# Two-layer diffusion trunk: softmax weights transposed in row halves, another spread of the convolution's taps, and later sums of a norm

## The chip, the cores and the metric

The kernel runs on one core of a Trainium2 chip. The metric is the time of one execution on the device in microseconds (us), the median of several runs. The engines are PE (TensorE: matmuls, with PEld for its weight loads), DVE (VectorE), ACT (ScalarE), POOL (GpSimd) and SP (SyncE, which issues the transfers here). Each runs its own list of instructions in order and waits for others by semaphores. Results of PE go to PSUM, eight banks of 128 partitions x 2 KB; everything else stands in SBUF.

## The reference

A trunk of two layers over 256 latent tokens and 256 context tokens, width 1024. Each layer mixes tokens by a convolution branch and an attention branch with gates, and then has a gated MLP. Cut to what matters:

```python
for l in range(DEPTH):                       # DEPTH = 2; the last layer: latent tokens alone
    h = modulate(rmsnorm(x, norm1_g[l]), sh1, sc1)
    p = h @ w_in[l]                          # columns: GLU, q, k, v, gates
    u = a * sigmoid(g)                       # a, g: halves of the GLU columns (512 each)
    u = dwconv1d(u, dw, dw_b)                # 31 taps per channel, along the tokens
    y_conv = silu(layernorm(u, ln_g, ln_b)) @ w_conv_out[l]
    s = concatenate([q @ k_window + bias, q @ k_ctx])     # 8 heads of 64
    y_attn = softmax(s) @ concatenate([v_window, v_ctx]) @ w_na_out[l]
    g_conv, g_attn = split(sigmoid(p_gate))
    x = x + g1 * ((g_conv * y_conv + g_attn * y_attn) @ w_out[l])
    h2 = modulate(rmsnorm(x, norm2_g[l]), sh2, sc2)
    x = x + g2 * conv_ffn(h2, w_up, dw3, dw3_b, w_down)
    # the same for the context tokens in layer one, with attention among themselves
return rmsnorm(x, final_norm_g)
```

## The kernel before, in words

Activations stand transposed, channels on the 128 partitions and tokens along the row: 256 latent tokens (`LAT`), then 256 context tokens (`CTX`). Layer one (index 0 in the code) has both, rows of T = 512; layer two (index 1, `last`) has T = 256. `S` is 256, `P` 128, `KD` 8, `KC` 4.

**Weights.** They come in units of 128 x 1024 from memory by SP (`wunit`, L155: tile `raw`, four buffers) and are split into a high part (ACT, L158, `whi`) and a low part (DVE, L159, `wlo`) in a rounded fp32 format, as is every activation. A product is three matmuls (`mm3`, L177 to L179: high x high, high x low, low x high). So ACT and DVE work for each unit that PE is to use, and a `raw` buffer is free when DVE has read it. SP's list also holds the units of the modulation's weights (`raw_unit`, L145) and two rows of the condition (`across`, tile `sb`, L243), which ACT puts through Silu (L245).

**Work between groups.** The main program on PE is a row of groups (8 k-steps of `mm3`). After halves or wholes of groups it calls `slot()`, which moves each generator in a list (`side`) one step on: the attention, the convolution's taps, its norm, the dots of the modulation on DVE (`ada_dots`, L261, custom instructions of 128 x 1024). The tile framework then decides each engine's order and its waits from the order in which the instructions were written, with `tc.issue_after` as extra constraints.

**Convolution.** `glu(j, ..)` writes tile `u` for channels j (four of them) and puts its 31 taps into the list `taps`. `conv_tap` is one DVE instruction (L576: `cb = u * w + cb`, 128 x 512 in layer one, 128 x 256 in layer two), 124 in each layer with the four first ones. `conv_run` gives `rate[0]` taps per slot. In layer one there were two `u` tiles, `us[j % 2]`, so `glu` first ran the taps that still read the tile it is to write. When the attention is over, `layer_norm` (L815) takes the rest in portions, then forms the mean (sum on POOL and DVE, a matmul with ones on PE, L832), subtracts it (L835), forms squares on ACT and their sums on DVE (L308, L312), lets PE sum over the channels (`rstd`, L326), DVE scale (`root`, L334), POOL take the power -0.5 (L336), PE spread it over the partitions (L341), and DVE and ACT normalise (L843 to L847). It yields between the steps, so its place on PE follows from the slots.

**Attention.** A step of `Attention.step` takes, in this order: the turn of the step before (L476), the values of the turn before that (L494), and the score products of the next pair of heads (L430), which use 64 rows of the array for each head, the two heads in the two row halves and in two banks. ACT and DVE then do the softmax (L448 to L454) into tiles `pp`, queries on partitions, keys along the row. The values need keys on partitions, so a *turn* transposes four `pp` tiles of 128 x 512: 16 transposes of 128 x 128 on PE (L484 for latent queries, L489 for context queries), into the banks `sc`, `sc`, `pt`, `main`, one for each `pp`, and four copies of 128 x 512 on ACT into `pT` (L485, L490). Then `values` (L502) multiplies by `V` into `po`, with 64 columns of the array for each head. Layer one has six turns (four latent, two context), layer two four: 160 transposes.

**The second norm of layer two.** After the residual (L883) the first four groups of the MLP run on `h2` without the factor of the norm (`plain`, L893 and L894), interleaved over k with its sums: at k = 2 `next(sums)` issues L326 and L334, at k = 4 `whole(sums)` the spread L341. The modulation of `h2` follows on DVE and ACT (L355 to L357), the first groups are scaled afterwards (L1000), and the next two groups read the modulated tiles. PE's work after L341 in these loops is what the modulation has for cover.

## Time and profile before

| what | value |
|---|---|
| median of three runs | 1130.06 us (1129.4 to 1134.78) |
| span of the profiled execution, from the first to the last instruction | 1127.4 us |
| granted TensorE clock, mean | 0.998 |
| layer one's attention, about | 80 to 203 us |
| layer two's turns | 813 to 861 us |
| layer two's second norm | 933 to 945 us |

The profile is of one execution. Its page gives busy times of the engines (PE's ends are modelled), the chain of work that ended last, followed back from the last instruction, and groups of instructions, each named by line, engine, operation and tile, with the count, busy time and mean in ns of one. `out<-in` are the program's tile names. In a timeline a row has start, length and name, and in brackets how long its engine stood idle before it and what released it. Two of the chain's kinds, `PEld` and `PE`, overlap: a weight load runs under the matmul before it. The execution's time outside the span isn't in the profile; 1130.06 and 1127.4 stand 2.7 us apart.

### The profile page before, as it was taken

The page shows a single profiled execution, that of the slowest core. Times are in us where ns is not written, and L with a number is a line of the kernel's source. Part 1 is how long each engine was busy: PE and PEld are TensorE (multiplying, and loading weights), DVE is VectorE, ACT ScalarE, POOL GpSimd, SP SyncE. Part 2 cuts the span into 40 slices and gives each one's busy share as a digit, 9 for nine tenths or more (in the row PEclk, how much of TensorE's full clock was granted, in tenths as well). Part 3 has the DMA queues.
Part 4 walks back from the last instruction along what each step waited for, and adds up shares of the span by engine and source line. Part 5 has one row for each costly group of instructions (what it writes and reads, how often), then busy time and mean ns, then how long its engine had stood idle before and what let it go on. Part 6 is the DMA issues. An engine that isn't in the chain of part 4 may idle for free.

```text
span 1127.4 us, 17780 instructions
## 1 busy us (share of the span) xinstructions
PE 1115.5 (99%) x6854; PEld 965.1 (86%) x6854; DVE 906.5 (80%) x1625; ACT 565.7 (50%) x937; POOL 17.2 (2%) x24
## 2 busy tenths in 40 slices
PE   9999999999999999999999999999999999999997
PEld 7678777787789988888888888989898999999997
DVE  4689999786778788888898555789996898988773
ACT  4347657542334543444334223544677667766642
POOL 0000000000000000000000000010000000000000
PEclk9999999999999999999999999999999999999999
DMA  8832231635734354545556656555533575665781
GB/s 325 310 100 89 92 117 38 200 99 198 248 120 145 110 170 133 184 152 155 165 181 205 214 188 197 176 194 174 154 109 120 180 247 175 187 193 182 213 274 57
DMA packets 53941, 190.83 MB, mean 169 GB/s; under 512 B 6240, under 2 KB 6496, under 8 KB 53856
## 3 DMA queue, kind: packets, MB, share of 16 engines
q1 hardware_dynamic: 53568, 189.65, 52.6%
q8 instruction: 54, 0.88, 0.3%
q14 instruction: 31, 0.25, 0.1%
q10 hardware_dynamic: 288, 0.04, 0.0%
HBM read 188.62 MB, written 1.05 MB: 168 GB/s over the span
## 4 chain that ended last, share of the span: by engine, by line
PE 85%; DVE 10%; DMA 2%; ACT 2%; issue 1%; POOL 0%; SPq 0%; DVEq 0%; ACTq 0%; POOLq 0%
PE main L177 25%; PE main L179 24%; PE main L178 24%; DVE cb L576 4%; PE main L629 4%; DVE wlo L159 2%; DMA raw<-in_wall 1%; PE sc L127 1%; PE sc L177 1%; PE sc L179 1%; PE sc L178 1%; PE po L200 1%; PE po L502 1%; DMA sb<-in_crow 1%; PE sc L430 0%
## 5 line engine op out<-in xcount | busy, mean ns | idle before, releaser
L177 PE MATMUL main<-h,whi 128*128 128x256 f32 (+1 forms) x1328 | 446.8, 337 | 0.0
L179 PE MATMUL main<-h,wlo 128*128 128x256 f32 (+1 forms) x1328 | 443.4, 335 | 0.5 <-DVE wlo L159 0.5
L178 PE MATMUL main<-h,whi 128*128 128x256 f32 (+1 forms) x1328 | 442.4, 333 | 0.0
L158 ACT CAST whi<-raw 128x1024 fp32r<-128x1024 f32 (+1 forms) x244 | 252.5, 1039 | 284.7 <-PE main L178 128.6
L159 DVE TENSOR_TENSOR wlo<-raw,whi 128x1024 fp32r<-128x1024 f32 (+1 forms) x244 | 293.7, 1209 | 113.3 <-ACT whi L158 108.6
L177 PEld LDWEIGHTS main<-h,whi 128*128 128x128 f32 x1328 | 249.5, 188 | 32.0 <-issue 3.9
L179 PEld LDWEIGHTS main<-h,wlo 128*128 128x128 f32 x1328 | 249.5, 188 | 28.9 <-DVE wlo L159 0.7
L178 PEld LDWEIGHTS main<-h,whi 128*128 128x128 f32 x1328 | 249.9, 188 | 28.1 <-issue 0.2
L576 DVE SCALAR_TENSOR_TENSOR cb<-u,par,cb 128x512 f32<-128x512 f32 (+1 forms) x240 | 140.6, 620 | 1.2
L261 DVE CUSTOM_DVE_ANT_0 t<-raw,sb,par 128x1024 bf16<-128x1024 f32 x100 | 126.9, 1280 | 1.4 <-ACT sb L245 1.2
L177 PE MATMUL main<-fh,whi 128*128 128x256 f32 (+1 forms) x386 | 123.0, 319 | 0.0
L178 PE MATMUL main<-fl,whi 128*128 128x256 f32 (+1 forms) x386 | 122.9, 319 | 0.0
L179 PE MATMUL main<-fh,wlo 128*128 128x256 f32 (+1 forms) x386 | 122.9, 318 | 0.0
L178 PEld LDWEIGHTS main<-fl,whi 128*128 128x128 f32 x386 | 72.7, 188 | 5.6
L177 PEld LDWEIGHTS main<-fh,whi 128*128 128x128 f32 x386 | 72.7, 188 | 5.6
L179 PEld LDWEIGHTS main<-fh,wlo 128*128 128x128 f32 x386 | 72.7, 188 | 5.5
L948 ACT ACTIVATE t<-main,par 128x512 f32<-128x512 f32 (+1 forms) x82 | 50.7, 669 | 35.3 <-PE main L179 35.3
L949 DVE SCALAR_TENSOR_TENSOR t<-main,par,t 128x510 f32<-128x510 f32 (+1 forms) x82 | 47.6, 616 | 8.2 <-ACT t L948 7.6
L952 DVE SCALAR_TENSOR_TENSOR t<-main,par,t 128x510 f32<-128x510 f32 (+1 forms) x82 | 46.6, 611 | 0.0
L356 ACT ACTIVATE h<-t,mod 128x256 fp32r<-128x256 f32 x56 | 25.2, 502 | 37.5 <-DVE t L355 37.4
L883 DVE SCALAR_TENSOR_TENSOR x<-main,mod,x 128x256 f32<-128x256 f32 x48 | 22.1, 480 | 23.6 <-PE main L179 23.4
L629 PE MATMUL main<-whi,h 128*128 128x512 f32 x128 | 40.6, 402 | 0.0
(217 smaller groups left out, 1198.0 us busy)
## 6 DMA issues: line engine op xcount, KB each, us to landing
raw<-in_wall SPq DMA_DIRECT2D x239, 512.0 KB, 4.2
raw<-in_wada SPq DMA_DIRECT2D x88, 512.0 KB, 4.4
bias<-in_bias_t SPq DMA_DIRECT2D x8, 640.0 KB, 4.4
row<-in_wada SPq DMA_DIRECT2D x8, 512.0 KB, 4.8
sb<-in_crow SPq DMA_DIRECT2D x5, 512.0 KB, 6.1
x<-in_xt SPq DMA_DIRECT2D x8, 256.0 KB, 4.6
raw<-in_wall SPq DMA_DIRECT2D x8, 256.0 KB, 6.8
out<-t SPq DMA_DIRECT2D x3, 256.0 KB, 2.1
```

The costliest lines, as they stand in the source:

```text
L158: act.copy(hi[:, c], r[:, c])
L159: dve.tensor_tensor(lo[:, c], r[:, c], hi[:, c].bitcast(F32), ALU.subtract)
L177: pe.matmul(ps, w[0], xh, start=start, stop=False)
L178: pe.matmul(ps, w[0], xl, start=False, stop=False)
L179: pe.matmul(ps, w[1], xh, start=False, stop=stop)
L261: dve.tensor_tensor_reduce(tmp().bitcast(BF16), r, v, 1.0, pr(l, BADA + n, 1), ALU.mult, ALU.add, mods[l][:, n, s : s + 1])
L356: high = act.activation(hi[:, c], y[:, c], AF.Identity, bias=b)
L576: dve.scalar_tensor_tensor(cb[j], src, w, cb[j], ALU.mult, ALU.add)
L629: pe.matmul(pv[t], h1[n == 1][k][:, c], w[n == 2][:, b], start=k + n == 0, stop=k == KD - 1 and n == 2)
L948: act.activation(c, pv_, AF.Identity, bias=pr(l, FDB + t, 1), scale=w[1])
L949: dve.scalar_tensor_tensor(c[:, :, 1:], pv_[:, :, : S - 1], w[0], c[:, :, 1:], ALU.mult, ALU.add)
L952: dve.scalar_tensor_tensor(c[:, :, : S - 1], pv_[:, :, 1:], w[2], c[:, :, : S - 1], ALU.mult, ALU.add)
```

## The change

1. **Turns.** Each 128 x 128 transpose becomes two of 64 x 128: the weights are rows 0 to 63 or 64 to 127 of `pp` and the moving operand is the 64 x 64 block of the identity on the same rows, so that 64 queries come out as 64 columns. The two halves of a block go to two banks, written in turn: a bank now holds one half of the queries for both heads of the pair (before: all 128 queries of one head). Both banks of a pair of heads get full together, after 16 halves, and then come their two copies. The copies are still four per turn with 512 columns, in stretches of 64. `pT` is one tile for both heads, two buffers, in place of two tiles with four.
2. **Taps.** Layer one has four `u` tiles (`NU_ = KC`), so `glu` forces no taps. `conv_run` counts with a fraction, 1.75 taps per slot in layer one in place of 2, and the norm takes 3 of the rest per slot in place of 5. Layer two keeps 3 and 6.
3. **Second norm.** In layer two `next(sums)` stands at k = 4 in place of 2, `whole(sums)` at k = 6 in place of 4.
4. **Scratch.** The program is built with `dynamic_dma_scratch_size=1024`, which leaves more of SBUF to the tiles.

In the compiled order layer one's mean L832 moves from place 1094 to 1334 on PE; 96 of these places are the added halves. Behind it come 27 matmuls up to L326 as before, and then 6 up to L341 (21 before).

```diff
-            pts = [self.eb.tile([P, 4, S], F32, tag="pT", bufs=4, name=nm("pT")) for _ in range(2)]
+            pT = self.eb.tile([P, 2, 4, S], F32, tag="pT", bufs=2, name=nm("pT"))
             for n, tags in enumerate((("sc", "sc"), ("pt", "main"))):
+                outs = [psum(t).rearrange("p (i s q) -> p i s q", i=2, s=4) for t in tags]
                 for i, pp in enumerate(pps[n]):
-                    pt = psum(tags[i])
+                    for s in range(4):
+                        src = s if what == LAT else s % 2 * 2 + s // 2
+                        for pt, r in zip(outs, HALF):
+                            pe.transpose(pt[:, i, s], sl(pp, src)[r], ident[r, r])
+                for pt, r in zip(outs, HALF):
                     if what == LAT:
-                        for kt in range(4):
-                            pe.transpose(sl(pt, kt), sl(pp, kt), ident)
-                        act.copy(pts[i][:, :, n * P : (n + 1) * P], pt.rearrange("p (k q) -> p k q", k=4))
+                        act.copy(pT[:, :, :, n * P + r.start : n * P + r.stop], pt)
                     else:
...
-                            pts[i][:, 2 * n + kt - kts[0], :], start=kt == kts[0], stop=kt == kts[-1],
+                            pT[:, i, 2 * n + kt - kts[0]], start=kt == kts[0], stop=kt == kts[-1],
...
-            NU_ = KC if last else 2
+            NU_ = KC
...
-            rate = [0]
+            rate = [0.0]
             def conv_run():
+                due = 0.0
                 while True:
-                    for _ in range(rate[0]):
+                    due += rate[0]
+                    while due >= 1:
+                        due -= 1
                         if taps:
                             conv_tap(*taps.pop(0))
                     yield
...
-                rate[0] = 3 if last else 2
+                rate[0] = 3 if last else 1.75
...
-                        for _ in range(6 if last else 5):
+                        for _ in range(6 if last else 3):
...
-                    if k == 2:
+                    if k == 4:
                         next(sums)
-                    if k == 4:
+                    if k == 6:
                         pb = whole(sums)
...
-    nc = bacc.Bacc("TRN2", target_bir_lowering=False, num_devices=1)
+    nc = bacc.Bacc("TRN2", target_bir_lowering=False, num_devices=1, dynamic_dma_scratch_size=1024)
```

More of the change, by code (lines that the diff above doesn't have):

```diff
@@ L476, in turn, with values @@
         def turn(self, what, its, pps):
-            pts = [self.eb.tile([P, 4, S], F32, tag="pT", bufs=4, name=nm("pT")) for _ in range(2)]
+            pT = self.eb.tile([P, 2, 4, S], F32, tag="pT", bufs=2, name=nm("pT"))
             for n, tags in enumerate((("sc", "sc"), ("pt", "main"))):
+                outs = [psum(t).rearrange("p (i s q) -> p i s q", i=2, s=4) for t in tags]
                 for i, pp in enumerate(pps[n]):
-                    pt = psum(tags[i])
+                    for s in range(4):
[3 more added lines that the diff above has]
+                for pt, r in zip(outs, HALF):
                     if what == LAT:
-                        for kt in range(4):
-                            pe.transpose(sl(pt, kt), sl(pp, kt), ident)
-                        act.copy(pts[i][:, :, n * P : (n + 1) * P], pt.rearrange("p (k q) -> p k q", k=4))
-                    else:
-                        for t in range(2):
-                            for kt in range(2):
-                                pe.transpose(pt[:, kt * S + t * P : kt * S + (t + 1) * P], sl(pp, 2 * t + kt), ident)
-                        act.copy(pts[i][:, 2 * n : 2 * n + 2, :], pt.rearrange("p (k q) -> p k q", k=2))
+                        act.copy(pT[:, :, :, n * P + r.start : n * P + r.stop], pt)
+                    else:
+                        to = pT[:, :, 2 * n : 2 * n + 2].rearrange("p i k (t q) -> p i (k t) q", t=2)
+                        act.copy(to[:, :, :, r], pt)
             js = [its[0][0]] if what == LAT else [it[0] for it in its]
-            self.pv.append((what, js, pts))
-        def values(self, what, js, pts, bank):
+            self.pv.append((what, js, pT))
+        def values(self, what, js, pT, bank):
             po = psum(bank)
```

## The prediction

> **What bounds the kernel now.** Views in this order: the page's head and chain, the windows of the stages that hold the ten turns, then the chain of waits in layer one.

> ```profile
> span 1127.4 us, 17780 instructions
> PE 1115.5 (99%) x6854; PEld 965.1 (86%) x6854; DVE 906.5 (80%) x1625; ACT 565.7 (50%) x937; POOL 17.2 (2%) x24
> PE 85%; DVE 10%; DMA 2%; ACT 2%; issue 1%; POOL 0%; SPq 0%; DVEq 0%; ACTq 0%; POOLq 0%
> ```

> TensorE is busy for 99% of the span, so time taken off PE counts in full wherever nothing else holds the stage. DVE's 10% of the chain says that somewhere it does (columns: PE, PEld, DVE, ACT, POOL, clock, DMA share, GB/s):

> ```profile
> core 0: us, PE busy (x) PEld busy (x) DVE busy (x) ACT busy (x) POOL busy (x), PEclk, DMA share, GB/s
> 84.00:112.00 28.00, 28.00 (x139) 22.18 (x137) 27.63 (x65) 20.06 (x39) 0.00 (x0) 1.00 0.27 89
> 112.00:140.00 28.00, 28.00 (x174) 22.05 (x173) 27.93 (x53) 20.20 (x45) 0.00 (x0) 1.00 0.32 99
> 140.00:170.00 30.00, 30.00 (x151) 23.71 (x151) 30.00 (x62) 17.79 (x31) 1.69 (x1) 1.00 0.37 110
> 170.00:200.00 30.00, 30.00 (x183) 23.46 (x183) 29.53 (x54) 24.05 (x57) 1.30 (x1) 1.00 0.12 36
> ...
> 872.00:900.00 28.00, 28.00 (x236) 27.95 (x236) 22.38 (x49) 16.92 (x36) 0.71 (x1) 1.00 0.58 188
> ```

> Between 84 and 200 us, layer one's attention, DVE idles 0.37 + 0.07 + 0.00 + 0.47 = 0.9 us in 116. Behind layer two's turns it has 28.00 − 22.38 = 5.6 us to spare. The chain of waits, and a line of PE's timeline, show where layer one's DVE work reaches PE:

> ```profile
> 198.98 0.75 DVE cb L576
> ...
> 200.73 1.15 DVE wlo L159
> ...
> 202.27 6.08 DMA sb<-in_crow
> ...
> 212.03 0.44 PE pt L224 x2
> ```

> ```profile
> 212.03 0.44 PE L224 MATMUL pt<-ident,t 128*128 128x128 f32 x2 [1.13 <-ACT t L217]
> ```

> A row of taps (L576), then the low part of a weight unit (L159), whose buffer SP's queue waits for; behind that the load of the context row, its two Silu on ACT, the copy L217 queued behind them, and PE's transpose L224, which stands 1.13 us. This is PE's longest stall. PE has only 1.13 us to give there before every microsecond gained earlier becomes waiting.

> **Edit 1, the turns.** It takes out 16 transposes in each of 10 turns and puts in 32 halves. Per turn before, from the chain of the first one: 0.87 / 8 = 109 ns each, 16 × 109 = 1.74 us.

> ```profile
> 102.85 0.87 PE sc L484 x8
> ```

> No row shows a half transpose. The nearest are the score products, which also run on row halves, into two banks (PE's, then the weight loads' timeline):

> ```profile
> 849.32 0.39 PE L430 MATMUL main<-qk,qk 64*128 64x512 f32 x1
> 849.55 0.39 PE L430 MATMUL pt<-qk,qk 64*128 64x512 f32 x1
> 849.55 0.39 PE L430 MATMUL main<-qk,qk 64*128 64x512 f32 x1
> 849.87 0.39 PE L177 MATMUL main<-h,whi 128*128 128x256 f32 x1
> ```

> ```profile
> 849.09 0.18 PEld L430 LDWEIGHTS pt<-qk,qk 64*128 64x128 f32 x1
> 849.09 0.18 PEld L430 LDWEIGHTS main<-qk,qk 64*128 64x128 f32 x1
> ```

> ```profile
> L326 PEld LDWEIGHTS pt<-one,ss 128*128 128x128 f32 x32 | 4.2, 190 | 1.5 <-DVE ss L312 1.0 <-PE sc L178 0.4
> L484 PEld LDWEIGHTS sc<-ident,pp 128*128 128x128 f32 x64 | 7.4, 141 | 0.8
> ```

> Both matmuls of a pair start together, both loads start together, and the pair steps by 849.55 − 849.32 = 0.23 us. So halves on different rows run side by side. A pair of half transposes moves 64 columns instead of 128: bound to the good side 109 / 2 + 3 ns = 57 ns, if it is the moving columns that set the 109. They seem to: the sums L326 move one column per load and take 0.79 / 8 = 99 ns each (row below), and a transposed load is 190 − 141 = 49 ns shorter than theirs, so about 50 ns. Middle bound: the pair costs what one transpose costs, 109 ns, if two loads of 50 ns don't overlap. Bad bound: the halves run one after the other at full price, 218 ns. I take 57, by the score rows, which show both kinds of overlap; the four instructions would then issue every 14 ns, which no row shows.

> [...]

> A turn then costs 16 × 57 = 0.91 us, 0.83 less. Against it: the values that follow 8 of the 10 turns (L502) run in 128 rows, so PE changes mode once more. Such a change shows above as 849.87 − 849.55 = 0.32 against 0.23, so 0.09 us. Where score products follow at once (the first turn of each layer) there is no extra change, but they wait for the copy of their bank, which now starts only when both banks of a pair are full:

> ```profile
> L485 ACT COPY pT<-sc 128x512 f32<-128x512 f32 x16 | 8.5, 587 | 0.0
> ```

> Two copies of 0.59 us stand between the turn and its banks, so I count these two turns at a gain of 0.2 at best and a loss of 0.4 (one rope copy comes between in layer two). Eight turns gain 0.74 each: five in layer one, three in layer two.

> *Layer one:* 5 × 0.74 = 3.7 us, and it doesn't pass. DVE's order in the changed program has the same L159 ahead of the context row, with one tap more before it (118 against 117), 0.75 us by the row above. DVE was full, so L224 comes 0.7 us later (bounds 0 and 1.0), and PE's stall there grows by about 4.4. Layer one: **+0.7**.

> *Layer two:* 3 × 0.74 = 2.2, less 0.2 for its first turn and 0.5 for weights that DVE splits just in time: **−1.5** (bounds −2.4 and 0).

> **Edit 2, tiles and taps.** Two more memsets on POOL, busy 2%, before any u is written, and no transfer: nothing. The tap count is the same 120; only their places change (counted above). But three leftover taps per slot instead of five, and no forced taps, put the convolution's norm later: its mean (L832) moves some 144 matmuls back on PE, into the groups of the next branch, where slots come twice as often. Before:

> ```profile
> 229.19 0.86 PE po L832 x2
> ...
> 236.32 0.79 PE pt L326 x8
> ...
> 242.09 0.44 PE po L341 x4
> ```

> ```profile
> 235.09 0.69 DVE L312 TENSOR_TENSOR ss<-ss,t 128x512 f32<-128x512 f32 x1
> 235.69 1.28 DVE L261 CUSTOM_DVE_ANT_0 t<-raw,sb,par 128x1024 bf16<-128x1024 f32 x1
> ```

> ```profile
> 237.39 1.99 POOL L336 TENSOR_TENSOR rs<-red,mhalf 128x4 f32<-128x4 f32 x1 [48.62 <-DVE red L334]
> ```

> Before, the squares end at 235.09 + 0.69 = 235.8, 6.6 us behind L832's start, and PE comes 7.1 behind it. After, one dot L261 more stands between the squares: 6.6 + 1.3 = 7.9 against about 7.1 to 7.2 of PE work, a stall of 0.7. Then from L326 to L341 PE had 21 products (4.9 us) over the power on POOL; after only 6, 6 × 0.23 = 1.4. The reduction L334 stands behind another L261 (0.5 us beyond the 0.79 of L326), then takes 0.2, and POOL 1.5 to 2.0: 2.2 to 2.7 against 1.4, a stall of 0.8 to 1.3. Together **+1.8** (bounds 0, if the products queued later have shrunk some other wait, and +4, if the dots find their weights late and L312 waits for two of them). What reads the normed tiles stands about 16 us of PE work behind, so nothing more is late. Where DVE has no dots the cover would be enough and the cost nothing.

> **Edit 3, the second norm's sums** go two steps of k back. PE's stall (first row) is covered: the sums come 24 products of 0.12 us later.

> ```profile
> 933.87 0.61 PE L326 MATMUL pt<-one,ss 128*128 128x1 f32 x4 [0.50 <-DVE ss L312]
> ```

> ```profile
> 937.48 0.22 PE po L341 x2
> ```

> ```profile
> 943.74 0.89 DVE L357 SCALAR_TENSOR_TENSOR h<-t,mod,h 128x256 fp32r<-128x256 f32 x2 [0.19 <-ACT h L356]
> ```

> But the modulation behind L341 also starts about 2.1 us later, and its last L357 ends near 944.6 + 2.1 = 946.7, while the groups that read it start three steps of k, 36 products of 0.12 us, behind L341 (937.7 + 4.3 = 942.0). In the changed order two groups take turns over k, so the last k is first read near 947. I take **−0.3** (bounds −0.5, all of the stall, and +2.2, if the last tile is waited for).

> **Edit 4, the smaller scratch for transfers.** Every load here is issued from SP; I cost it at nothing, and no cover hides it.

> **Sum:** 0.7 − 1.5 + 1.8 − 0.3 = +0.7 on a span of 1127.4, so 1128.1. The median of the runs, 1130.06, stands 2.7 above the span: **1130.8 us**. A change under 0.5% (5.7 us) can't be told from none here.

> **The rivals.**

> *The whole gain passes* (30%). If L224 isn't held by DVE in the changed program, because the context row is loaded earlier or fewer taps per slot bring L159 forward, layer one keeps 3.7 us and may lose up to the 1.13 of stall too. −3.7 − 1.1 − 2.2 − 0.3 and, with the norm's waits covered, 0 for edit 2: −7.3, **1122.8**. For it: POOL and ACT have room, and 1.75 taps leave a quarter of one per slot to other DVE work. Against it: DVE's 0.9 us of idle time, and the same work in front of L159.

> *The halves run one after the other* (12%): slower. Place: the 16 pairs of each turn; price 218 − 109 = 109 ns a pair, 1.74 us a turn. Layer one's 10.5 us less 1.1 of the stall is 9.4, layer two's 7.0, with 0.8 of mode changes, 1.8 and −0.3: +18.7, **1149**. It decides from a pair of about 145 ns on, where the sum passes +5.7. For it: both halves write the same 64-column stretch of two banks, and none of the shown pairs is a transpose. Against it: the score pairs.

> *The pair costs what the whole cost* (10%): no gain, 0.7 + 0.7 of mode changes + 1.8 − 0.3 = +2.9, **1133**. [...]

> *The norm of layer one costs more* (6%): the dots, loaded in turn with the weights, hold L312 and L334, and sh and sl come late for the products that read them; +4 there and 16 us of cover used up by about 3 more: 0.7 − 1.5 + 7 − 0.3 = +5.9, **1136**. It decides once DVE in that stretch is over 90% busy.

> **How the numbers follow.** The forecast has 42%, about 1126 to 1134 by its own bounds. Faster by over 0.5%: the whole gain passing, 30%. Slower: serial halves 12%, the larger norm 6%, a little of the forecast's upper bound 3%: 21%. Within 0.5%: 49%. The range of 8 in 10 reaches down to 1121 and up to 1141, leaving out the serial halves and what is below the full gain.

> **What would show it.** Half transposes 57 ns a pair, a turn near 0.9 us (edit 1's price); L224's stall at 4 to 6 us, with DVE still full before 200 us (swallowed); stalls of about 1 us each at L326 and L341 of the convolution's norm; no stall before the sums near 936. I am wrong if L224 comes earlier than 212, or a turn takes over 1.7 us.

## The result, and the profile after

The changed kernel takes 1143.64 us (median of 5 runs, 1142.8 to 1149.65), the kernel before 1131.22 in the same comparison: a ratio of 1.012, interval 1.0094 to 1.0146. It is slower by some 12 us; forecast were 1130.8, and the range ended at 1141.

The page of the profiled execution, head and chain:

```profile
span 1147.9 us, 18102 instructions
PE 1124.2 (98%) x7014; PEld 965.9 (84%) x7014; DVE 908.4 (79%) x1625; ACT 564.9 (49%) x937; POOL 18.2 (2%) x26
PE 79%; DVE 14%; ACT 4%; DMA 2%; issue 2%; SPq 0%; POOL 0%; DVEq 0%; ACTq 0%; POOLq 0%
```

The chain's share of PE has fallen by 6 points, those of DVE and ACT have risen by 4 and 2: PE waits for both. This execution lost some 3 us at the start, so the readings below are from a second profile of the same kernel (run e4_again: 1143.87 us, span 1142.1). Lines of kernel.py stand 1 to 4 lower there: L485 is the half transpose (L484 and L489 before), L488 its copy, L836 the mean (L832), L839 the centring (L835).

The starts of the same instructions of PE in both profiles say where the time went (the difference is the second profile's start less the one before):

| instruction on PE | before, us | changed, us | difference |
|---|---|---|---|
| L127, end of the start-up | 17.71 | 18.19 | +0.5 |
| L502, values in layer one | 180.53 | 179.72 | -0.8 |
| L502, values after the last context turn | 194.34 | 196.85 | +2.5 |
| L224 | 212.03 | 214.92 | +2.9 |
| L200, products of the modulation behind the norm | 298.04 | 309.30 | +11.3 |
| L326, first norm of layer two | 737.19 | 749.96 | +12.8 |
| L502, last values of layer two | 868.07 | 881.45 | +13.4 |
| L179, behind layer two's second norm | 973.49 | 988.12 | +14.6 |

These are differences of two single executions and add up to 14.6 us, where the medians stand 12.4 apart. The largest part, 8.4 us, lies between 215 and 309 us; in between PE has the same products in both kernels. Windows of the kernel before and then of the changed one (columns as in the prediction):

```profile
230.00:260.00 30.00, 30.00 (x137) 24.44 (x136) 27.93 (x44) 13.98 (x21) 1.99 (x1) 1.00 0.39 120
260.00:300.00 40.00, 40.00 (x221) 30.01 (x220) 22.66 (x39) 9.30 (x13) 0.00 (x0) 1.00 0.63 212
```

```profile
170.00:200.00 30.00, 27.57 (x195) 20.34 (x193) 29.69 (x54) 22.73 (x53) 1.65 (x1) 0.94 0.14 42
200.00:230.00 30.00, 29.73 (x148) 22.50 (x147) 24.31 (x37) 16.59 (x24) 0.00 (x0) 1.00 0.60 211
230.00:260.00 30.00, 30.00 (x130) 24.22 (x130) 9.67 (x13) 7.42 (x11) 0.00 (x0) 1.00 0.40 123
260.00:300.00 40.00, 34.40 (x173) 24.82 (x173) 31.68 (x57) 12.40 (x19) 2.00 (x1) 0.96 0.47 155
```

From 230 to 260 us DVE does 9.7 us of work where it did 27.9, while PE is full and seems fine. The bill comes in the next window: PE idles 5.6 us of 40, and its clock falls to 0.96; with the 1.7 us that this costs (below) that is most of the 8.4. DVE's timeline of the changed kernel, then SP's:

```profile
252.50 1.23 DVE L159 TENSOR_TENSOR wlo<-raw,whi 128x1024 fp32r<-128x1024 f32 x1 [4.36 <-ACT whi L158]
266.45 2.48 DVE L839 SCALAR_TENSOR_TENSOR cb<-po,cb 128x512 f32<-128x512 f32 x4 [12.72 <-PE po L836]
```

```profile
253.75 17.79 SPq L145 DMA_DIRECT2D raw<-in_wada  x2
271.65 0.37 SPq L155 DMA_DIRECT2D raw<-in_wall  x1
```

DVE has reached the centring of the convolution's norm and stands 12.7 us, because PE comes to the mean that late. Everything behind the centring in DVE's list stands with it. By then SP had run ahead and filled the four `raw` buffers: two with dots (loads at 237.6 and 253.8) that DVE reads behind the centring, from 269.4 on, and two with units of the modulation's products L200 (242.6 and 248.2) that PE reads at 270.5. So no buffer came free, and SP stood from 254 to 271 us (the first row of SP's list holds two loads, issued at 253.75 and 271.22, with the wait between them):

```profile
SPq L145 <- PE sc L200: 18.4, 3, 17.1
```

It is the L200 on PE that ends the wait; in the kernel before, the same pair was loaded at 256.4 and 257.5, and while PE had yet to read it, a split on DVE freed another buffer, so that the next pair came ahead: its first unit was loaded at 265.9, its second at 269.7, as soon as PE had read the first of the old pair. Here the next pair is loaded at 276.1 and 280.8, and PE gets to it too early. What PE waited for between 100 and 310 us, in the changed kernel (total, times, longest):

```profile
PE sc L200 <- DMA raw<-in_wada: 4.4, 2, 3.8
PE pt L485 <- ACT pp L472: 2.2, 1, 2.2
PE sc L430 <- ACT pT L488: 1.1, 2, 0.9
PE po L341 <- POOL rs L336: 0.8, 1, 0.8
PE main L177 <- DVE g L874: 0.3, 1, 0.3
PE pt L224 <- ACT t L217: 0.3, 1, 0.3
```

The first row is that pair. L341 is the stall that was forecast at 0.8 to 1.3. The forecast stall at L224 is nearly gone: PE had lost the time before, at L485 and L430.

After two of these stalls the clock is granted at half. Windows of the changed kernel around the stall of L485 and the one of L200:

```profile
192.00:196.00 4.00, 1.63 (x28) 1.04 (x26) 3.96 (x7) 3.50 (x13) 1.65 (x1) 1.00 0.00 0
196.00:200.00 4.00, 3.97 (x25) 2.17 (x25) 3.81 (x6) 3.97 (x7) 0.00 (x0) 0.57 0.00 0
```

```profile
280.00:284.00 4.00, 0.64 (x8) 0.16 (x8) 4.00 (x8) 1.34 (x2) 0.00 (x0) 1.00 0.54 153
284.00:288.00 4.00, 3.46 (x14) 2.25 (x15) 4.00 (x6) 2.27 (x4) 0.00 (x0) 0.59 0.80 246
```

4 us at 0.57 and 4 us at 0.59 each lose 4 x 0.42 = 1.7 us of PE work beyond the stall itself; PE is shown busy all the while.

Last, the turn. PE's timeline has pairs of halves:

```profile
179.20 0.22 PE L485 MATMUL main<-ident,pp 64*128 64x64 f32 x1
179.26 0.22 PE L485 MATMUL pt<-ident,pp 64*128 64x64 f32 x1
179.26 0.22 PE L485 MATMUL main<-ident,pp 64*128 64x64 f32 x1
```

The two halves of a pair start together and the next pair 0.06 us later; the whole turn has its first half at 178.59 and its last pair at 179.57, 0.98 / 15 = 65 ns a pair. The halves are nearly as fast as forecast: the second turn of layer one takes 1.14 us up to the values (112.46 to 113.60) where it took 1.84 (112.00 to 113.84). What became of the 0.70 us, on ACT in the kernel before and in the changed one:

```profile
111.97 1.05 ACT L158 CAST whi<-raw 128x1024 fp32r<-128x1024 f32 x1
113.03 1.28 ACT L591 ACT_TABLE_LOAD   x1
114.33 0.60 ACT L591 ACTIVATE t<-main 128x512 f32<-128x512 f32 x1
114.82 1.07 ACT L485 COPY pT<-sc 128x512 f32<-128x512 f32 x2
```

```profile
112.94 1.04 ACT L158 CAST whi<-raw 128x1024 fp32r<-128x1024 f32 x1
114.00 1.28 ACT L595 ACT_TABLE_LOAD   x1
115.29 0.60 ACT L595 ACTIVATE t<-main 128x512 f32<-128x512 f32 x1
115.79 1.07 ACT L488 COPY pT<-sc 128x512 f32<-128x512 f32 x2
```

```profile
116.42 1.46 PE L430 MATMUL sc<-qk,qk 64*128 64x256 f32 x12 [0.87 <-ACT pT L488]
```

ACT does the same list in the same time, one split, a table load and a sigmoid ahead of the copies; before, PE's score products began at 115.72, as the copies of their banks came to an end. The 0.70 us become a wait (0.87 us by the profile; ACT's list also starts 1.0 us later here, 0.5 of it by the later start of PE). At this turn the copies weren't late because two banks fill together; they were never waiting for PE.

### The profile page after: what moved, and what is told of

Read it like the earlier page. It is cut to its first block, busy times and chain, and to the rows that moved or that the text cites. A ratio compares the mean times of both kernels' runs of the same rounds, so it can differ in the third digit from the quotient of the medians.

```text
span 1147.9 us, 18102 instructions
## 1 busy us (share of the span) xinstructions
PE 1124.2 (98%) x7014; PEld 965.9 (84%) x7014; DVE 908.4 (79%) x1625; ACT 564.9 (49%) x937; POOL 18.2 (2%) x26
## 4 chain that ended last, share of the span: by engine, by line
PE 79%; DVE 14%; ACT 4%; DMA 2%; issue 2%; SPq 0%; POOL 0%; DVEq 0%; ACTq 0%; POOLq 0%
PE main L177 23%; PE main L179 23%; PE main L178 22%; DVE cb L577 6%; PE main L633 4%; DVE wlo L159 3%; PE sc L127 1%; PE sc L177 1%; PE sc L179 1%; PE sc L178 1%; ACT whi L158 1%; PE po L200 1%; DMA raw<-in_wada 1%; DMA sb<-in_crow 1%; DVE sc L448 1%
## 5 line engine op out<-in xcount | busy, mean ns | idle before, releaser
L177 PE MATMUL main<-h,whi 128*128 128x256 f32 (+1 forms) x1328 | 446.5, 337 | 0.0
L179 PE MATMUL main<-h,wlo 128*128 128x256 f32 (+1 forms) x1328 | 442.8, 335 | 1.1 <-DVE wlo L159 1.1
L178 PE MATMUL main<-h,whi 128*128 128x256 f32 (+1 forms) x1328 | 442.3, 334 | 0.1
L159 DVE TENSOR_TENSOR wlo<-raw,whi 128x1024 fp32r<-128x1024 f32 (+1 forms) x244 | 293.3, 1208 | 111.4 <-ACT whi L158 106.6
L177 PEld LDWEIGHTS main<-h,whi 128*128 128x128 f32 x1328 | 249.4, 188 | 32.2 <-issue 4.4
L179 PEld LDWEIGHTS main<-h,wlo 128*128 128x128 f32 x1328 | 249.3, 188 | 29.7 <-DVE wlo L159 1.5
L178 PEld LDWEIGHTS main<-h,whi 128*128 128x128 f32 x1328 | 249.8, 188 | 28.6 <-DVE h L357 0.5
L261 DVE CUSTOM_DVE_ANT_0 t<-raw,sb,par 128x1024 bf16<-128x1024 f32 x100 | 127.0, 1279 | 8.4 <-DMA raw<-in_wada 6.9
L177 PE MATMUL main<-fh,whi 128*128 128x256 f32 (+1 forms) x386 | 123.0, 319 | 0.0
L178 PE MATMUL main<-fl,whi 128*128 128x256 f32 (+1 forms) x386 | 122.9, 319 | 0.0
L179 PE MATMUL main<-fh,wlo 128*128 128x256 f32 (+1 forms) x386 | 122.9, 318 | 0.0
L178 PEld LDWEIGHTS main<-fl,whi 128*128 128x128 f32 x386 | 72.7, 188 | 5.6
L179 PEld LDWEIGHTS main<-fh,wlo 128*128 128x128 f32 x386 | 72.7, 188 | 5.6
L177 PEld LDWEIGHTS main<-fh,whi 128*128 128x128 f32 x386 | 72.7, 188 | 5.5
L356 ACT ACTIVATE h<-t,mod 128x256 fp32r<-128x256 f32 x56 | 25.3, 502 | 37.8 <-DVE t L355 37.7
```

What stands on the lines that cost most here:

```text
L159: dve.tensor_tensor(lo[:, c], r[:, c], hi[:, c].bitcast(F32), ALU.subtract)
L177: pe.matmul(ps, w[0], xh, start=start, stop=False)
L178: pe.matmul(ps, w[0], xl, start=False, stop=False)
L179: pe.matmul(ps, w[1], xh, start=False, stop=stop)
L261: dve.tensor_tensor_reduce(tmp().bitcast(BF16), r, v, 1.0, pr(l, BADA + n, 1), ALU.mult, ALU.add, mods[l][:, n, s : s + 1])
L356: high = act.activation(hi[:, c], y[:, c], AF.Identity, bias=b)
```

## The experiments

Theory A: the loss is edit 2's, which puts the norm so late on PE that DVE stands at it, and the buffers and SP's queue behind DVE. Rival B: the turns cost it.

**e1_turns**: the kernel before with edit 1 alone.

> The kernel before with the half transposes alone. Theory A (the norm of layer one's convolution, moved later by the taps, costs the time): no loss of note here, since the norm keeps its place; the ratio to the kernel before is 0.996 to 1.002 (1126 to 1133 us), a turn costs about 1.0 us (62 ns a pair) in place of 1.74. Rival B (the turns themselves cost it: the copies that wait for two full banks, the changes of mode, the stall before a context turn): 1.006 or more, 1138 us and up.

1136.97 us, ratio 1.0048 (1.0025 to 1.0071): neither. The halves alone lose 5 us, too much for A, too little for B, though the interval reaches into B's range. In its profile L502 at 180.53 stands 1.2 us earlier against the start-up's end (+1.8 less +3.0), and then PE waits 1.1 us inside the last context turn (L485 for the weights that ACT normalises), and the clock is at 0.79 over the next 8 us. At the second norm of layer two it waits 2.8 us, with 0.57 over 8 us behind. The ten runs spread from 1133.1 to 1142.6.

**e2_taps**: the kernel before with edits 2 and 4 alone.

> The kernel before with four u tiles, 1.75 taps per slot, 3 leftover taps per slot and the small scratch, and nothing else. Theory A: most of the loss is here, 1.007 to 1.011 (1139 to 1143 us), with the stalls at L341 and at the modulation's products L200 between 260 and 300 us, DVE idle for over 10 us ahead of the centring of the norm, and the clock granted lower behind the stalls. Rival B: under 1.003.

1141.43, ratio 1.0087 (1.0057 to 1.0117): as theory A has it. The waits of PE between 200 and 310 us, with no half transpose in the kernel:

```profile
PE sc L200 <- DMA raw<-in_wada: 5.3, 2, 4.1
PE po L341 <- POOL rs L336: 0.8, 1, 0.8
```

**e3_sums**: the kernel before with edit 3 alone.

> The kernel before with the second norm's sums at k = 4 and k = 6 alone. Both theories: 0.9995 to 1.0005, a gain of the stall of 0.5 us at the sums, given back by small stalls at the modulated tiles behind them. Rival C (the sums carry the 2 us that layer two lost behind 868 us): 1.0015 to 1.003.

1130.33, ratio 0.999 (0.9974 to 1.0007): no difference that shows, and rival C falls. In its profile the wait of 0.50 us at the sums is gone, and a new one of 0.55 us stands 30 us behind them, at a weight that DVE has yet to split:

```profile
966.19 0.39 PE L179 MATMUL main<-h,wlo 128*128 128x256 f32 x1 [0.55 <-DVE wlo L159]
```

All eight profiles of kernels with edit 3 have this wait (0.54 to 0.57 us), and none of the six without.

**e4_again**: the changed kernel, a second profile.

> The changed kernel once more, for a second profile. If the first 2.8 us that the first profile lost before 21 us at half the granted clock belong to the change, they are here again; if they belong to that execution alone, the span is about 1141 us with clock 0.993, as the other runs show. The stalls near 197, 280 to 288 us are here again by all theories.

1143.87, span 1142.1: the start-up costs +0.5 here. The 2.8 us belong to that execution; e1_turns had them too, e5_turns_sums not at all.

**e5_turns_sums**: edits 1 and 3.

> The changed kernel without the taps' part: half transposes and later sums alone. Theory A2 (the turns' gain is lost where score products wait for the copies, and what is over is lost at stalls after which the clock is granted at half for some us; the norm of layer two was one of those in the run with the turns alone): 2 to 4 us less than the turns alone, 1.000 to 1.003, no half clock behind 940 us. Rival (the turns cost by themselves, whatever stands behind them): 1.0045 to 1.006, as the turns alone.

1135.21, ratio 1.0034 (1.0018 to 1.0051). Between the two expectations: 1.8 us less than the turns alone, with the half clock behind 940 us gone (the mean granted clock of the profiled execution is 0.996 in place of 0.990), but the intervals overlap. Without the taps' part the change loses 4 us in place of 12.

**e6_five**, **e7_three** and **e8_u4** take edit 2 apart by the portion of leftover taps and the tiles:

```diff
# e6_five, from the changed kernel
-                        for _ in range(6 if last else 3):
+                        for _ in range(6 if last else 5):
# e7_three, from the kernel before
-                        for _ in range(6 if last else 5):
+                        for _ in range(6 if last else 3):
# e8_u4, from the kernel before (with edit 4, and the fraction's code at 2 taps per slot)
-            NU_ = KC if last else 2
+            NU_ = KC
```

> The changed kernel with five leftover taps per slot in the norm in place of three, all else changed. The mean of the norm then stands 84 places earlier on PE and 6 dots ahead of the centring on DVE in place of 10. Theory A (the dots and with them SP's queue stand behind the late norm): the stalls at the modulation's products L200 (4 to 5 us, and the half clock behind) go, ratio 1.003 to 1.006. Rival (any norm among the branch's groups costs the same): 1.010 or more.

> The kernel before with three leftover taps per slot in place of five alone (mean 48 places later on PE, 6 dots ahead of the centring). If the three alone carry edit 2's loss: 1.006 to 1.009. By theory A the loss comes from the place among the dots, which takes the other parts too: 1.000 to 1.003.

> The kernel before with four u tiles and the small scratch alone: two taps per slot, five leftover taps. The mean stands 36 places later, 4 dots ahead of the centring as before. Theory A: 0.998 to 1.002. If the tiles themselves (their places in memory, the taps no longer forced) cost something: 1.004 and more.

e7 gave 1130.89 (ratio 1.0005, 0.9988 to 1.0022) and e8 1132.34 (1.0012, 0.9997 to 1.0026), both as theory A has it: neither part alone costs anything that shows. e6 gave 1140.03 (1.0076, 1.0049 to 1.0102), too slow for its expectation: no wait at L200 is left, but PE waits 1.6 us for a split weight at 289 us, whose load stood 3.9 us in SP's queue until PE read a unit for L200. SP's longest wait there was 10.1 us, for a dot on DVE, and it is as long in e8, which loses nothing. So with the other parts a norm 60 places late still costs something; how the halves and the fewer taps take part in that was not taken apart.

**e9_early**: a longer stall, put into the kernel before.

```diff
-                    if k == 2:
+                    if k == 0:
                         next(sums)
-                    if k == 4:
+                    if k == 2:
                         pb = whole(sums)
```

1133.69, ratio 1.0024 (1.0005 to 1.0043). PE's timeline and the clock's windows:

```profile
934.98 0.61 PE L326 MATMUL pt<-one,ss 128*128 128x1 f32 x4 [2.43 <-DVE ss L312]
937.53 0.69 PE L341 MATMUL po<-ident,rs 128*128 128x128 f32 x2 [0.75 <-POOL rs L336]
```

```profile
932.00:936.00 4.00, 1.57 (x13) 1.36 (x12) 3.13 (x7) 3.97 (x8) 0.14 (x1) 1.00 0.89 316
936.00:940.00 4.00, 3.25 (x19) 3.04 (x18) 2.67 (x6) 2.27 (x5) 1.47 (x1) 0.62 0.78 269
```

The half clock follows the stall, in a kernel whose instructions are those of before; the rival's clock of 1.00 falls, though its time (1.0025 or less) fits. The price was put too high: 2.43 - 0.50 + 0.75 = 2.7 us of new stall and 4 x 0.38 = 1.5 us of clock are 4.2 in the profiled execution (span 1131.9 against 1127.4), but 2 us between the medians. The runs spread from 1131.1 to 1139.0, and the stall that the edit lengthens is not the same in every execution: 0.50 us in the profile of before, 1.3 in e7's and 1.0 in e8's, which leave this place as it was.

**e10_nodots**: the changed kernel with no dots during the norm.

```diff
                         yield
-                    pace[0] = 1.0
+                    pace[0] = 0.0
```

> The changed kernel with no dots of the modulation issued while layer one's convolution norm runs (pace 0 in place of 1 there; they follow later). Theory A (the dots stand behind the late norm on DVE, their loads stand in SP's queue behind buffers that they hold, and the modulation's products L200 wait for loads behind those): no stall at L200 and no half clock between 280 and 300 us, SP's longest wait there under 8 us in place of 17.8; 5 to 8 us less than the changed kernel, 1.004 to 1.008. Rival (the place of the norm alone costs it): 1.010 to 1.012.

1151.5, ratio 1.0177 (1.0148 to 1.0206): slower still. L200 waits no more, but PE's waits between 200 and 400 us read

```profile
PE sc L179 <- DVE wlo L159: 5.5, 1, 5.5
PE main L177 <- ACT whi L158: 3.9, 2, 2.2
```

Part of the second (1.7 us) is at 287 us, near the old place: a weight's load had stood in SP's queue for 9.4 us, again until PE read a unit for L200. The first is at 382 us, behind the dots that were put off: seven of them run one behind the other on DVE from 360.7 to 369.1. From 372 to 388 us PE idles 8.4 us of 16, at a mean clock of 0.57. So the total says little about the norm, but its stretch can be read: from L224 to the products L200 of the table, the same work on PE takes 86.0 us in the kernel before, 94.4 in the changed one and 90.8 here. Without the dots the norm's stretch gets back 3.6 of 8.4 us, and the wait moves to the next thing that the queue holds; the expectation, which made the dots the whole cause and put no price on where they would go, was wrong by at least 11 us. What is left of theory A is the lateness of the norm.

**e11_eight**: all of the change, but the norm back at its old place, by one number.

```diff
-                        for _ in range(6 if last else 3):
+                        for _ in range(6 if last else 8):
```

> The changed kernel with eight leftover taps per slot in the norm in place of three: the four tiles, 1.75 taps per slot, the half transposes and the later sums stay, and the mean of the norm stands where it stood in the kernel before (place 1190, 96 of them the halves), with 4 dots ahead of the centring. Theory A (edit 2's loss is the norm's place): 1.002 to 1.005, as the half transposes with the later sums alone (1.0034), DVE not idle for over 3 us ahead of the centring. Rival (fewer taps per slot or the tiles lose it before the norm): 1.008 or more.

1134.94, ratio 1.0019 (1.0004 to 1.0034). One number takes back 9 us by the medians, 11 by the ratios, with the four tiles, the 1.75 taps, the halves and the later sums in place; the stretch from L224 to L200 takes 85.9 us, as before the change. The group row of the centring (busy, mean ns, idle before it) in the kernel before, the changed kernel and e11:

```profile
L835 DVE SCALAR_TENSOR_TENSOR cb<-po,cb 128x512 f32<-128x512 f32 x4 | 2.5, 684 | 1.6 <-PE po L832 1.6
```

```profile
L839 DVE SCALAR_TENSOR_TENSOR cb<-po,cb 128x512 f32<-128x512 f32 x4 | 2.5, 684 | 12.7 <-PE po L836 12.7
```

```profile
L839 DVE SCALAR_TENSOR_TENSOR cb<-po,cb 128x512 f32<-128x512 f32 x4 | 2.5, 683 | 1.6 <-PE po L836 1.6
```

The kernels in order of the mean's place on PE (less the halves):

| kernel | place of the mean | DVE's wait at the centring, us | DVE busy, 230 to 260 us | ratio |
|---|---|---|---|---|
| before | 1094 | 1.6 | 27.9 | 1 |
| e11_eight, with halves | 1094 | 1.6 | 23.7 | 1.0019 |
| e8_u4 | 1130 | 4.4 | 20.9 | 1.0012 |
| e7_three | 1142 | 1.6 | 19.9 | 1.0005 |
| e6_five, with halves | 1154 | 4.4 | 14.6 | 1.0076 |
| e2_taps | 1238 | 12.7 | 8.0 | 1.0087 |
| changed kernel | 1238 | 12.7 | 9.7 | 1.012 |

It is no straight line and not the wait at the centring alone: 36 and 48 places are nearly free, 60 with the halves cost 6 us against e11, 144 cost 11 with them (against e11) and 10 without them.

**e12_values_first**: e5 with other work in place of the stall in the last context turn.

```diff
+            if soft and soft[0][0] == CTX and not self.todo:
+                for work in pv:
+                    self.values(*work, "po")
+                pv = []
             for what, its, pps in soft:
```

> Half transposes and later sums alone, with the values of layer one's last attention step issued ahead of its last turn, so that PE works 1.9 us while ACT finishes the softmax. The stall of 1.1 us inside that turn and the half clock behind it go. Theory D (DVE holds layer one: the time gained is taken again by the wait at L224): L224 starts no earlier than 212.5 us, its stall is over 1.5 us, ratio 1.002 to 1.0045, no gain against 1.0034. Rival (the stall and its half clock are on the path): L224 1.5 to 2 us earlier, 1.0015 to 1.002.

1134.86, ratio 1.0019 (1.0006 to 1.0031), which doesn't part it from e5. The wait in the turn is gone, PE is 1.8 us ahead of the kernel before in the gate's products behind it (194.4 against 196.2), and then it waits for the last copies of that turn:

```profile
200.24 3.17 PE L507 MATMUL sc<-pT,V 128*64 128x256 f32 x16 [2.78 <-ACT pT L495]
```

L224 starts at 213.39, no earlier than 212.5 as theory D asked, but without the stall of over 1.5 us that theory D put there: ACT's copies take the gain, one step earlier, and the clock is at 0.79 over 8 us behind them. What PE gains in layer one is waited off somewhere before 213 us.

## Why the prediction was wrong

| term of the sum | forecast, us | measured, us (differences of the first table) |
|---|---|---|
| layer one up to L224 | +0.7 | 2.9 - 0.5 = +2.4 |
| the convolution's norm | +1.8 (0 to 4) | 11.3 - 2.9 = +8.4 |
| up to layer two's first norm | 0 | +1.5 |
| layer two's turns | -1.5 | +0.6 |
| its second norm | -0.3 | +1.2 |

*The step that failed most is edit 2's norm.* I counted what PE would wait for inside the norm's own chain. Of that the power came as forecast (L341 stalls 0.8 us) and the squares did not (L326 doesn't stall: the 27 products ahead of it were counted, but not the 16 of L200 that now stand there too, so that PE has 8.3 us to work where I had 7.1). I then wrote that nothing more is late. What I didn't ask was how long DVE itself would stand at the centring when the mean comes 144 matmuls later, and what is taken in the meantime: 12.7 us, the dots of two units behind it with their `raw` buffers, two more held for PE, SP's one queue, and at the end PE's modulation products, some 27 us after DVE began to stand. I had looked at what delays L312, and not at what waits behind L839. e11_eight shows that the place is what costs, e2_taps that the halves aren't needed for it, e10_nodots that the dots carry less than half of it in the norm's own stretch. The rest of the way, from DVE's stand over the buffers and the queue to PE, is read from the traces; no run changes the number of buffers or the order of the queue. The rival of 1136 had the right place, too small a price, and a wrong mark (DVE over 90% busy; from 230 to 260 us it was idle for 20 of 30).

*The price of the halves was right* (57 ns a pair forecast, 61 to 66 measured; no run shows the 3 ns that the 57 has above half of 109), and that layer one would swallow the gain was right too. But where the gain goes failed twice. In layer two I let three turns keep 0.74 us each, since values lie between the turn and the next score products. They don't cover ACT. At the second turn (831 us in the kernel before) the difference between the two profiles falls by 0.6 at the values and rises by 0.6 at the score products behind them: on ACT the copies come 2.5 us behind the turn's start in place of 0.9, behind a rope copy (L757) that waits 1.3 us for DVE. The first turn loses 0.5 (forecast 0.2), the third keeps its 0.6. The last one takes 1.76 us up to the values, hardly less than the 1.84 before, and the last values L502 wait 0.7 us for a bank that DVE reads. I had priced the copies at 0.59 us without the queue ahead of them, which the trace of before shows. In layer one the stall came at a context turn in place of L224, and behind its 2.2 us stood the half clock (0.57 from 196 to 200 us). There PE waits for ACT's softmax, and ACT had waited for DVE:

```profile
188.74 0.48 ACT L467 ACTIVATE pp<-sc,mx 128x256 f32<-128x256 f32 x1 [5.53 <-DVE mx L462]
```

So it is DVE that holds layer one, as I had it, but at the softmax ahead of the turn. This stall is 1.1 us in e1 and e5, which have the old taps, 2.2 us in all five profiles with the new taps and the halves, and absent in e2: the two edits add up there, where I had counted one tap at L224. (L224, which I called PE's longest stall in the kernel before, is so only behind the program's first 2 us, where L127 waits 1.8.)

*The clock was missing as a term.* I read 1.00 in every stretch of before and took it as given. The half clocks behind the stalls at 195 and 284 us (0.57 and 0.59 over 4 us) cost an estimated 1.7 us each.

*Edit 3 at -0.3*: alone it shows no difference (0.999, 0.9974 to 1.0007), in keeping with it, but I looked for its price at the modulated tiles, and it is the wait of 0.55 us for a split weight behind them. That wait is about half of the +1.2 there; the rest of it and the +1.5 at layer two's first norm are not settled. At the latter PE waits 0.9 to 1.6 us at L326 in each profile of a kernel with halves, where a weight unit reaches ACT about 1 us later, and 0.1 to 0.3 us in those without; by which way the halves delay that load was not tried.

*The chances.* Slower had 21%, most of it for halves that run one after the other, which the pairs rule out at 61 to 66 ns each. No row spoke for a gain of the whole 7 us, for I had read myself that DVE was full; 30% was too much.

## What to carry to other kernels

When a step is moved later on one engine, find the instruction on each other engine that waits for it, work out how long that engine will now stand there, and list everything behind it in that engine's order: buffers that it frees, then the load queue that waits for those buffers. A stretch in which an engine of a full pipeline suddenly does a third of its work can be where a later stall begins, as here, though nothing waits there yet. And before time saved on the busiest engine is counted, look at when the next thing that it needs is ready: if another engine's list sets that, the saving becomes a wait, and in this kernel a wait of about 2 us often cost more than its length (2.2 us at L485, and an estimated 1.7 us by the half clock behind it).

## What the runs showed of the hardware

**Half transposes on the two row halves run side by side** also at 64 columns: in the changed kernel's turn at 181.4 us (first profile) the two loads of a pair start within 0.01 us of each other in the timeline, and so do its two matmuls; from the first to the last pair it is 62 ns a pair for the loads and 66 for the matmuls, where one whole transpose took 109.

**The clock after a stall.** The time from one PE instruction's start to the next one's, and the clock over the 8 us from the latter:

| run, place | start to start, us | clock over 8 us |
|---|---|---|
| changed (e4), L430 at 116 | 1.25 | 1.00 |
| before, L224 at 212 | 1.51 | 1.00 |
| e7, second norm | 1.57 | 1.00 |
| e11, L326 at 744 | 1.61 | 0.79 |
| changed (e4), L326 at 750 | 1.75 | 1.00 |
| changed, first profile, L326 at 754 | 1.92 | 0.79 |
| e6, L177 at 289 | 1.99 | 1.00 |
| e2, second norm | 2.07 | 0.79 |
| e9, second norm | 2.71 | 0.79 |
| e1, second norm | 3.10 | 0.57 |
| e1, inside a turn | 1.36 | 0.79 |
| changed (e4), inside a turn | 2.47 | 0.79 |

0.79 over 8 us is 3.4 us at half, 0.57 is 6.8; in the first profile of the changed kernel the clock reads 0.50 from 754.91 to 758.32 us, and 1.00 in the 3.41 us before and behind. Outside a turn nothing followed up to 1.57 us in these rows, from 2.07 on it did in each of them, and between the two it went either way. Where a stall falls may have a part in that. In the first profile of the changed kernel the clock changes at 14.2, 21.0, 198.5, 201.9, 287.3, 294.1, 754.9, 758.3 and 1140.6 us: the later eight stand 2, 54, 55, 80, 82, 217, 218 and 330 steps of 3.413 us behind the first. For the other profiles, such steps counted on from a half clock that their windows show are an estimate. By it the 1.75 us of e4's L326 are split between two steps (counted from 284.7 us, PE idles 1.0 us in the one that ends at 752.4 us); the 1.92 us of the first profile lie in one (1.6 us idle up to 754.9), and only there the half clock followed. It doesn't account for every row: in e6 a step with 1.6 us idle (286.5 to 289.9, counted from 194.3) was followed by the full clock, 1.00 over 8 us, and in e11 one with 1.3 (741.8 to 745.2, counted from about 199) by 0.79. Inside a turn 1.36 us was enough in e1; no run shows why. This can also spread the runs: whether a stall near 2 us costs 1.7 us more differed between the two profiles of the changed kernel.
